# Where the moving operands of TensorE begin, modulo 128 bytes, in a two-layer fp32 block on one Trainium2 core

## The chip, the core and the metric

The kernel runs on one core of one Trainium2 chip (trn2). The metric is device microseconds of one execution: 2106.06 us is the median of three runs of the kernel before (2105.8 to 2108.58).

## The reference

Two layers on 256 tokens of width 2048, all in float32. Layer 0 is a convolution and pooling mixer and a swiglu, layer 1 a short-convolution mixer and a swiglu; an RMS norm ends it. Nearly all of the work is matrix products with weights that are each used once:

```python
def swiglu(h, w_gate, w_up, w_down):
    return (jax.nn.silu(h @ w_gate) * (h @ w_up)) @ w_down

    for i in range(DEPTH):
        ...
        if i % 2 == 0:
            h = h + conv_pool_mixer(h, ...)
        else:
            h = h + short_conv_mixer(h, ...)
        h = h + swiglu(rms_norm(h, ffn_norm[i]), w_gate[i], w_up[i], w_down[i])
    return rms_norm(h, final_norm)
```

The first mixer projects to 3072 features, runs a 31-tap causal convolution with a layer norm over 1024 of them and pooled averages over 1024, and projects back. The second projects to 6144 features, gates and convolves with 3 taps, and projects back. A swiglu has 5632 hidden features.

## The kernel before, in words

Activations lie with features on the partitions: a chunk is 128 features by 256 tokens, and the residual `h` has 16 chunks. The weights come as 128 x 128 blocks in the order of their use, from one array `in_wall`, in transfers of up to 16 blocks into the tiles `w`.

Every product is made in split precision. A weight piece of 8 blocks is rounded by ScalarE into `hi` (L114), and the rest, `w - hi`, goes into `lo` (L121, on VectorE, for part of the first mixer on GpSimd). `hi` and `lo` have 6 buffers each, and pieces are prepared 4 ahead of their use. An activation chunk is split alike by `split` (L193 to L200): it lies in 2 KB of a partition, 256 high values and then 256 low ones. For one weight block and one chunk, `product` issues in one of two forms:

- wide (all but the first mixer and the last chunk of the output): `hi` by all 512 columns of the chunk (L163), then `lo` by the 256 high ones (L164). This is called a pair here.
- narrow (the first mixer, and the last output chunk): `hi` by the 256 high values (L166), `hi` by the 256 low ones (L167), `lo` by the 256 high ones (L168). This is called a triple.

Each product loads its block of weights (512 bytes of each partition) into TensorE (PEld in the profile) and streams the chunk past it. Four tiles are streamed, the moving operands:

- `xs`, 16 chunks of normed input. It lives through the whole program and is written anew for each of the four stages that read it: the first mixer (M0; there it also takes the pooled branch's output, L200 from the pooling product), the first swiglu (F0), the second mixer (M1), the second swiglu (F1).
- `cat`, 8 chunks: in M0 first the pooled averages, later the layer-normed branch.
- `y`, 22 chunks: half of a swiglu's hidden features, filled and read twice in each swiglu.
- `z`, 16 chunks: the second mixer's gated values.

The stages follow each other: M0 (512 triples by `xs`, 144 by `cat`), F0 (`xs` 704 pairs, `y` 352, `xs` 704, `y` 352), M1 (`xs` 768, `z` 256), F1 (as F0, with the last 22 products of `y` as triples). In M0 the convolution's taps, the pooling and the layer norm run on VectorE, ScalarE and GpSimd beside the products, fed in by queues that count products. M0's last projection reads `cat` and waits for the layer norm; that norm's last steps stand in VectorE's order among the preparations of weights.

Tiles are placed by pools, one after the other in each partition: `h`, `xs`, then the four buffers of `w`, the six of `hi`, the six of `lo`, small ones, and last the tiles of the stage. So a tile that grows pushes those behind it.

Of the kernel before, what the change touches and what calls it, by code (L numbers as in the profile page):

```python
# [12 lines left out]
F32R = mybir.dt.float32r  # L13
# [4 lines left out]
P = 128  # L18
T = 256
D = 2048  # L20
NC = D // P
DC = 1024
NA = DC // P
FF = 5632
NF = FF // P
NH = NF // 2
# [46 lines left out]
WARM = 9  # L73

KEEP = 8

POOL_SPLIT = range(96, 24 * NC + 16 + 7 * NC + 8)

# [6 lines left out]
def block_kernel(ctx: ExitStack, tc: tile.TileContext, xT: bass.AP, xtok: bass.AP, vec: bass.AP, wall: bass.AP, out: bass.AP):  # L85
    nc = tc.nc
    const = ctx.enter_context(tc.tile_pool(name="const", bufs=1))
    act = ctx.enter_context(tc.tile_pool(name="act", bufs=1))
# [35 lines left out]
    def next_block():  # L124
        b, i = cursor
        at = UNIT_AT[PIECES[i][0]] + PIECES[i][1]
        if b == at + PIECES[i][2]:
            ready.pop(i)
            i, at = i + 1, b
        for j in range(i, i + LOOK + 1):  # L130
            prepare(j)
        if i + LOOK < len(PIECES):
            for u in range(PIECES[i + LOOK][0] + 1, PIECES[i + LOOK][0] + AHEAD + 1):
                fetch(u)
        cursor[:] = [b + 1, i]
        hi, lo = ready[i]
        o = (b - at) * P
        return hi[:, o : o + P], lo[:, o : o + P]
# [8 lines left out]
    def tick():  # L147
        for name, q in queues.items():
            credit[name] = credit[name] + 1.0 if q else 0.0
            while q and credit[name] >= PACE[q[0][0]]:  # L150
                cost, step = q.popleft()
                credit[name] -= PACE[cost]
                step()

    def drain():
        while any(queues.values()):
            for q in queues.values():
                if q:
                    q.popleft()[1]()

    def product(acc, hi, lo, x, first, last, wide):
        if wide:
            nc.tensor.matmul(acc, hi, x, start=first, stop=False, skip_group_check=True)  # L163
            nc.tensor.matmul(acc[:, T:], lo, x[:, :T], start=False, stop=last, skip_group_check=True)  # L164
        else:
            nc.tensor.matmul(acc[:, :T], hi, x[:, :T], start=first, stop=False)  # L166
            nc.tensor.matmul(acc[:, :T], hi, x[:, T:], start=False, stop=False)  # L167
            nc.tensor.matmul(acc[:, :T], lo, x[:, :T], start=False, stop=last)  # L168

    def matmul_chunks(xs, ks, n=1, wide=False, behind=None):  # L170


        accs = [ps.tile([P, 2 * T], F32, name="acc") for _ in range(n)]
        for i, k in enumerate(ks):
            first, last = i == 0, i == len(ks) - 1
            for acc in accs:
                hi, lo = next_block()
                product(acc, hi, lo, xs[:, k, :], first, last, wide)
                tick()
            if behind is not None:  # L180
                behind(k)
        return accs
# [10 lines left out]
    def split(dst, src, scale=None):  # L193

        if scale is None:
            nc.scalar.copy(dst[:, :T], src)
            nc.vector.tensor_tensor(out=dst[:, T:], in0=src, in1=dst[:, :T], op=ALU.subtract)
        else:
            nc.scalar.activation(dst[:, :T], src, AF.Copy, scale=scale)
            nc.vector.scalar_tensor_tensor(out=dst[:, T:], in0=src, scalar=scale, in1=dst[:, :T], op0=ALU.mult, op1=ALU.subtract)  # L200
# [4 lines left out]
    def col(name, i):  # L205
        return v[:, VECS[name] + i : VECS[name] + i + 1]

    identity = v[:, VECS["identity"] :]
    h = act.tile([P, NC, T], F32, name="h")
    xs = act.tile([P, NC, 2 * T], F32R, name="xs")  # L210
    ones = const.tile([P, P], F32, name="ones")
    nc.gpsimd.memset(ones, 1.0)

# [14 lines left out]
    def rsqrt_of(*totals, scale, halves=False, st=None):  # L228
# [9 lines left out]
        if halves:  # L238

            idle = ps.tile([P, P], F32, name="idle", tag="acc")  # L240
            with tc.issue_after(mm.ins):
                for _ in range(KEEP):
                    nc.tensor.matmul(idle, ones, ones, start=True, stop=True)  # L243
# [27 lines left out]
    class Norm:  # L271


        def __init__(self, gain, final=False):
            self.gain, self.final = gain, final
            self.sums = []

        def add(self, c):
# [6 lines left out]

        def scale(self, c):
            if not self.final:
                split(xs[:, c, :], h[:, c, :], col(self.gain, c))

        def square(self, c):  # L290
            if c == 0:
# [16 lines left out]
    def project(src, ks, norm=None, wide=False, narrow_end=False):  # L308

        for n in range(NC):  # L310
            if narrow_end and n == NC - 1:
                wide = False
            (acc,) = matmul_chunks(src, ks, wide=wide)
            if wide:
                t = phase[0].tile([P, T], F32, name="cross", bufs=3)
                nc.scalar.copy(t, acc[:, T:])
                nc.vector.tensor_tensor(out=h[:, n, :], in0=h[:, n, :], in1=t, op=ALU.add)
            nc.vector.tensor_tensor(out=h[:, n, :], in0=acc[:, :T], in1=h[:, n, :], op=ALU.add)  # L318
            if norm is not None:
                norm.add(n)  # L320

    def scaled(acc, r, name, wide=False):
        if not wide:
            s = (phase[0] if name == "pv" else tmp).tile([P, T], F32, name=name, bufs=2)
            nc.vector.tensor_tensor(out=s, in0=acc[:, :T], in1=r, op=ALU.mult)
            return s
        s = summed(acc, name)
        nc.vector.tensor_tensor(out=s, in0=s, in1=r, op=ALU.mult)
        return s


    norm = Norm("mix_norm_e")
    nc.sync.dma_start(v[:, :NC], vec[:, :NC])

    def load(at, n):
# [30 lines left out]
    every = range(NC)  # L366
    with tc.tile_pool(name="m0", bufs=1) as m0, tc.tile_pool(name="ps_side", bufs=2, space=PSUM) as ps_side:
# [1 line left out]
        a_in = m0.tile([P, NA, pad + T], F32, name="a_in")  # L369
        nc.gpsimd.memset(a_in[:, :, :pad], 0.0)  # L370
        conv = m0.tile([P, NA, T], F32, name="conv")
        cat = m0.tile([P, NA, 2 * T], F32R, name="cat")
        total = m0.tile([P, 2, T], F32, name="total")

        sides, prods, state = {}, {}, {}
# [156 lines left out]

        project(xs, POOL_CHUNKS)
        drain()
        norm = Norm("ffn_norm0")
        project(cat, range(NA), norm)

    def swiglu(norm, following):
        with tc.tile_pool(name="ffn", bufs=1) as fp:
            phase[0] = fp  # L540
            y = fp.tile([P, NH, 2 * T], F32R, name="y")
            r = None
            for half in range(2):
                for f in range(NH):
                    (acc_g,) = matmul_chunks(xs, every, wide=True)
                    (acc_u,) = matmul_chunks(xs, every, wide=True)
                    if r is None:
                        r = norm.rstd()
                    gate = scaled(acc_g, r, "gate", True)
                    up = scaled(acc_u, r, "val", True)  # L550
                    nc.scalar.activation(gate, gate, AF.Silu)
                    nc.vector.tensor_tensor(out=up, in0=up, in1=gate, op=ALU.mult)
                    split(y[:, f, :], up)
                project(y, range(NH), following if half else None, wide=True, narrow_end=half and following.final)
# [1 line left out]
    x0.close()  # L556


    after = Norm("mix_norm_o")
    swiglu(norm, after)  # L560


    norm = Norm("ffn_norm1")
    with tc.tile_pool(name="m1", bufs=1) as m1:
        phase[0] = m1
        z = m1.tile([P, NC, 2 * T], F32R, name="z")
        pad = SW - 1
        r = None
        for c in range(NC):
            (acc_c,) = matmul_chunks(xs, every, wide=True)  # L570
            (acc_v,) = matmul_chunks(xs, every, wide=True)
            if r is None:
                r = after.rstd()
            cg = scaled(acc_c, r, "gate", True)
            vv = scaled(acc_v, r, "val", True)
            cv = m1.tile([P, pad + T], F32, name="cv", bufs=2)
            nc.gpsimd.memset(cv[:, :pad], 0.0)
            nc.vector.tensor_tensor(out=cv[:, pad:], in0=cg, in1=vv, op=ALU.mult)
            wc = VECS["conv_w_o"] + c * SW
            co = m1.tile([P, T], F32, name="co", bufs=2)  # L580
            nc.vector.tensor_scalar(out=co, in0=cv[:, :T], scalar1=v[:, wc : wc + 1], scalar2=None, op0=ALU.mult)
            for k in range(1, SW):
                nc.vector.scalar_tensor_tensor(out=co, in0=cv[:, k : k + T], scalar=v[:, wc + k : wc + k + 1], in1=co, op0=ALU.mult, op1=ALU.add)
            (acc_b,) = matmul_chunks(xs, every, wide=True)
            bg = scaled(acc_b, r, "pv", True)
            nc.vector.tensor_tensor(out=bg, in0=bg, in1=co, op=ALU.mult)
            split(z[:, c, :], bg)
        project(z, every, norm, wide=True)


    last = Norm("final_norm", final=True)
    swiglu(norm, last)
    halves = rsqrt_of(*last.sums, scale=1.0 / D, halves=True)
    with tc.tile_pool(name="fin", bufs=1) as fin:

# [90 lines left out]
```

## Time and profile before

| | |
|---|---|
| median of three runs | 2106.06 us (2105.8 to 2108.58) |
| profiled execution | 2103.73 us, its span 2102.0 us |
| TensorE clock granted, mean | 0.997 of full |
| matmuls, weight loads | 12584 each |
| transfers | 395.53 MB, mean 188 GB/s |

The page gives busy time by engine, the chain of work that ended last, and groups of instructions by line and tile; times are microseconds unless marked ns. Matmuls are pipelined, and the duration of one reaches into the next. The view of one tile in a stretch gives for each line the count, the shortest, median and longest duration in ns, and the start of the first and of the last, in us from the span's start. The view of stretches gives for each engine the busy time and, in brackets, its instructions, then the clock, the share of the DMA engines and GB/s. The chain of waits gives start, duration and instruction.

### The profile page before, as it was taken

How to read it: one execution, taken by the hardware profiler on the slowest of the kernel's cores; microseconds unless marked ns; L12 is line 12 of the kernel's file. 1: busy time of each engine (PE TensorE's matmuls, PEld its weight loads, DVE VectorE, ACT ScalarE, POOL GpSimd, SP SyncE). 2: the span in 40 equal slices, each digit the busy share in tenths (PEclk: the TensorE clock that was granted, in tenths of full speed). 3: DMA queues.
4: the chain of work that ended last, by engine and by line, in shares of the span. 5: the costliest groups of instructions: out<-in, count | busy, mean ns of one | idle time of the engine just before them, and what ended most of it. 6: DMA issues, size and time to landing. Idle time of an engine off the chain costs nothing.

```text
span 2102.0 us, 31608 instructions
## 1 busy us (share of the span) xinstructions
PE 2079.1 (99%) x12584; PEld 1855.8 (88%) x12584; DVE 1383.4 (66%) x1979; ACT 1060.9 (50%) x1571; POOL 200.6 (10%) x180
## 2 busy tenths in 40 slices
PE   8999999999999999999999999999999999999998
PEld 8999988888888888888888888888888888888887
DVE  6888866666556666666777777666666556666654
ACT  7776654444444444454444445554444444444453
POOL 3985200000000000011000001100000000000011
PEclk9999999999999999999999999999999999999999
DMA  8554455555555555555555555555555555555551
GB/s 326 187 191 168 158 184 197 183 198 182 194 185 188 193 187 194 183 196 182 183 198 182 198 183 193 180 189 198 183 196 184 189 192 183 198 182 199 182 192 68
DMA packets 56884, 395.53 MB, mean 188 GB/s; under 512 B 6432, under 2 KB 7200, under 8 KB 9760
## 3 DMA queue, kind: packets, MB, share of 16 engines
q1 hardware_dynamic: 56736, 393.52, 52.4%
q8 instruction: 98, 1.61, 0.3%
q14 instruction: 50, 0.41, 0.1%
HBM read 391.39 MB, written 2.10 MB: 187 GB/s over the span
## 4 chain that ended last, share of the span: by engine, by line
PE 98%; DMA 1%; DVE 1%; ACT 0%; SPq 0%; issue 0%; DVEq 0%; ACTq 0%
PE acc L163 57%; PE acc L164 30%; PE acc L166 4%; PE acc L168 4%; PE acc L167 4%; DMA rows<-in_xtok 0%; DMA h<-in_xT 0%; DVE res L603 0%; ACT hi L114 0%; PE st L237 0%; PE st L268 0%; DVE lo L121 0%; SPq L104 0%; ACT conv L475 0%; PE idle L243 0%
## 5 line engine op out<-in xcount | busy, mean ns | idle before, releaser
L114 ACT CAST hi<-w 128x1024 fp32r<-128x1024 f32 (+1 forms) x740 | 776.1, 1050 | 975.3 <-PE acc L163 621.0
L121 DVE TENSOR_TENSOR lo<-w,hi 128x1024 fp32r<-128x1024 f32 (+1 forms) x691 | 845.2, 1224 | 639.5 <-ACT hi L114 635.3
L163 PE MATMUL acc<-xs,hi 128*128 128x512 f32 x3584 | 1243.3, 391 | 0.0
L164 PE MATMUL acc<-xs,lo 128*128 128x256 f32 x3584 | 1004.7, 280 | 0.0
L163 PEld LDWEIGHTS acc<-xs,hi 128*128 128x128 f32 x3584 | 670.4, 187 | 146.2
L164 PEld LDWEIGHTS acc<-xs,lo 128*128 128x128 f32 x3584 | 678.1, 189 | 0.1
L163 PE MATMUL acc<-y,hi 128*128 128x512 f32 x1386 | 485.2, 393 | 0.0
L164 PE MATMUL acc<-y,lo 128*128 128x256 f32 x1386 | 386.4, 279 | 0.0
L163 PEld LDWEIGHTS acc<-y,hi 128*128 128x128 f32 x1386 | 259.4, 187 | 61.7
L164 PEld LDWEIGHTS acc<-y,lo 128*128 128x128 f32 x1386 | 259.9, 187 | 0.4
L298 POOL TENSOR_TENSOR sumsq<-sumsq,sq 128x256 f32<-128x256 f32 x56 | 58.8, 1050 | 1599.1 <-ACT sq L296 1599.1
L166 PE MATMUL acc<-xs,hi 128*128 128x256 f32 x512 | 144.0, 284 | 5.2 <-ACT hi L114 4.2
L167 PE MATMUL acc<-xs,hi 128*128 128x256 f32 x512 | 143.6, 283 | 0.0
L168 PE MATMUL acc<-xs,lo 128*128 128x256 f32 x512 | 141.3, 284 | 0.1
L121 POOL TENSOR_TENSOR lo<-w,hi 128x1024 fp32r<-128x1024 f32 x49 | 118.7, 2441 | 43.1 <-PE acc L167 34.3
L166 PEld LDWEIGHTS acc<-xs,hi 128*128 128x128 f32 x512 | 98.1, 192 | 6.2 <-ACT hi L114 5.0
L167 PEld LDWEIGHTS acc<-xs,hi 128*128 128x128 f32 x512 | 98.2, 192 | 0.0
L168 PEld LDWEIGHTS acc<-xs,lo 128*128 128x128 f32 x512 | 96.5, 192 | 0.5 <-DVE lo L121 0.5
L163 PE MATMUL acc<-z,hi 128*128 128x512 f32 x256 | 89.6, 393 | 0.0
L188 ACT COPY cross<-acc 128x256 f32<-128x256 f32 x224 | 80.6, 360 | 0.0
L164 PE MATMUL acc<-z,lo 128*128 128x256 f32 x256 | 71.3, 279 | 0.0
L318 DVE TENSOR_TENSOR h<-acc,h 128x256 f32<-128x256 f32 x112 | 47.2, 423 | 18.9 <-PE acc L168 13.2
(134 smaller groups left out, 1198.6 us busy)
## 6 DMA issues: line engine op xcount, KB each, us to landing
w<-in_wall SPq DMA_DIRECT2D x365, 1024.0 KB, 4.8
w<-in_wall SPq DMA_DIRECT2D x7, 512.0 KB, 7.7
rows<-in_xtok SPq DMA_DIRECT2D x2, 1024.0 KB, 7.9
h<-in_xT SPq DMA_DIRECT2D x7, 256.0 KB, 7.3
out<-res SPq DMA_DIRECT2D x2, 512.0 KB, 2.8
out<-res SPq DMA_DIRECT2D x2, 384.0 KB, 2.8
v<-in_vec SPq DMA_DIRECT2D x1, 260.0 KB, 6.7
h<-in_xT SPq DMA_DIRECT2D x2, 128.0 KB, 2.3
```

Source lines behind the costliest of these rows:

```text
L114: nc.scalar.copy(hi[:, : n * P], w)
L121: engine.tensor_tensor(out=lo[:, : n * P], in0=w, in1=hi[:, : n * P], op=ALU.subtract)
L163: nc.tensor.matmul(acc, hi, x, start=first, stop=False, skip_group_check=True)
L164: nc.tensor.matmul(acc[:, T:], lo, x[:, :T], start=False, stop=last, skip_group_check=True)
L166: nc.tensor.matmul(acc[:, :T], hi, x[:, :T], start=first, stop=False)
L167: nc.tensor.matmul(acc[:, :T], hi, x[:, T:], start=False, stop=False)
L168: nc.tensor.matmul(acc[:, :T], lo, x[:, :T], start=False, stop=last)
L188: nc.scalar.copy(t, acc[:, T:])
L298: nc.gpsimd.tensor_tensor(out=self.sums[0], in0=self.sums[0], in1=sq, op=ALU.add)
L318: nc.vector.tensor_tensor(out=h[:, n, :], in0=acc[:, :T], in1=h[:, n, :], op=ALU.add)
```

## The change

Each of the four moving tiles gets 32 more elements (128 bytes) in each partition, and what the program reads and writes is a view in it that begins some bytes in: 0 or 32, one number for each tile and stage (`XS_M0` 32, `Y_F0`, `Y_F1` and `Z_M1` 32, all others 0). The views of `xs` for the stages lie in one tile, so M0's and F0's overlap shifted by 32 bytes.

```diff
+XS_M0 = 32
+XS_F0 = 0
+XS_M1 = 0
+XS_F1 = 0
+Y_F0 = 32
+Y_F1 = 32
+Z_M1 = 32
+CAT = 0
...
-    xs = act.tile([P, NC, 2 * T], F32R, name="xs")
+    xs_room = act.tile([P, NC * 2 * T + 32], F32R, name="xs")
+
+    def moving(room, at, n):
+
+        return room[:, at // 4 : at // 4 + n * 2 * T].rearrange("p (c t) -> p c t", c=n)
...
-        def __init__(self, gain, final=False):
+        def __init__(self, gain, at=0, final=False):
             self.gain, self.final = gain, final
+            self.xs = moving(xs_room, at, NC)
...
-                split(xs[:, c, :], h[:, c, :], col(self.gain, c))
+                split(self.xs[:, c, :], h[:, c, :], col(self.gain, c))
...
-    norm = Norm("mix_norm_e")
+    norm = Norm("mix_norm_e", XS_M0)
+    xs = norm.xs
...
-        cat = m0.tile([P, NA, 2 * T], F32R, name="cat")
+        cat = moving(m0.tile([P, NA * 2 * T + 32], F32R, name="cat"), CAT, NA)
...
-            y = fp.tile([P, NH, 2 * T], F32R, name="y")
+            y = moving(fp.tile([P, NH * 2 * T + 32], F32R, name="y"), at, NH)
...
-        z = m1.tile([P, NC, 2 * T], F32R, name="z")
+        z = moving(m1.tile([P, NC * 2 * T + 32], F32R, name="z"), Z_M1, NC)
```

The order of the instructions on each engine and the semaphores that they wait for are the same in both programs. What differs is the addresses. These are the bytes in each partition at which the tiles begin in the built programs; `hi`'s first buffer stands for all weights, since the buffers of `hi` and `lo` lie 4096 bytes apart. Distance is moving operand minus weights.

| operand | before | after | distance mod 128, before | after | distance mod 512, before | after |
|---|---|---|---|---|---|---|
| `hi` | 101696 | 101824 | | | | |
| `xs` in M0 | 36160 | 36192 | 0 | 32 | 0 | 416 |
| `xs` in F0, M1, F1 | 36160 | 36160 | 0 | 0 | 0 | 384 |
| `cat` | 184672 | 184800 | 32 | 32 | 32 | 32 |
| `y`, `z` | 159136 | 159296 | 96 | 0 | 96 | 128 |

More of the change, by code (lines that the diff above doesn't have):

```diff
@@ L534, in block_kernel, with swiglu @@
         drain()
-        norm = Norm("ffn_norm0")
+        norm = Norm("ffn_norm0", XS_F0)
         project(cat, range(NA), norm)
-    def swiglu(norm, following):
+    def swiglu(norm, following, at):
         with tc.tile_pool(name="ffn", bufs=1) as fp:
             phase[0] = fp
-            y = fp.tile([P, NH, 2 * T], F32R, name="y")
+            y = moving(fp.tile([P, NH * 2 * T + 32], F32R, name="y"), at, NH)
             r = None
@@ L544, in swiglu @@
                 for f in range(NH):
-                    (acc_g,) = matmul_chunks(xs, every, wide=True)
-                    (acc_u,) = matmul_chunks(xs, every, wide=True)
+                    (acc_g,) = matmul_chunks(norm.xs, every, wide=True)
+                    (acc_u,) = matmul_chunks(norm.xs, every, wide=True)
                     if r is None:
@@ L556, in block_kernel @@
     x0.close()
-    after = Norm("mix_norm_o")
-    swiglu(norm, after)
-    norm = Norm("ffn_norm1")
+    after = Norm("mix_norm_o", XS_M1)
+    swiglu(norm, after, Y_F0)
+    norm = Norm("ffn_norm1", XS_F1)
     with tc.tile_pool(name="m1", bufs=1) as m1:
         phase[0] = m1
-        z = m1.tile([P, NC, 2 * T], F32R, name="z")
+        z = moving(m1.tile([P, NC * 2 * T + 32], F32R, name="z"), Z_M1, NC)
         pad = SW - 1
@@ L569, in block_kernel @@
         for c in range(NC):
-            (acc_c,) = matmul_chunks(xs, every, wide=True)
-            (acc_v,) = matmul_chunks(xs, every, wide=True)
+            (acc_c,) = matmul_chunks(after.xs, every, wide=True)
+            (acc_v,) = matmul_chunks(after.xs, every, wide=True)
             if r is None:
@@ L583, in block_kernel @@
                 nc.vector.scalar_tensor_tensor(out=co, in0=cv[:, k : k + T], scalar=v[:, wc + k : wc + k + 1], in1=co, op0=ALU.mult, op1=ALU.add)
-            (acc_b,) = matmul_chunks(xs, every, wide=True)
+            (acc_b,) = matmul_chunks(after.xs, every, wide=True)
             bg = scaled(acc_b, r, "pv", True)
@@ L591, in block_kernel @@
     last = Norm("final_norm", final=True)
-    swiglu(norm, last)
+    swiglu(norm, last, Y_F1)
     halves = rsqrt_of(*last.sums, scale=1.0 / D, halves=True)
```

## The prediction

> **What bounds the kernel now.** I read the page first: the busy shares, the chain that ended last, and the costliest groups.
>
> ```profile
> span 2102.0 us, 31608 instructions
> PE 2079.1 (99%) x12584; PEld 1855.8 (88%) x12584; DVE 1383.4 (66%) x1979; ACT 1060.9 (50%) x1571; POOL 200.6 (10%) x180
> PE 98%; DMA 1%; DVE 1%; ACT 0%; SPq 0%; issue 0%; DVEq 0%; ACTq 0%
> L114 ACT CAST hi<-w 128x1024 fp32r<-128x1024 f32 (+1 forms) x740 | 776.1, 1050 | 975.3 <-PE acc L163 621.0
> L163 PE MATMUL acc<-xs,hi 128*128 128x512 f32 x3584 | 1243.3, 391 | 0.0
> L163 PE MATMUL acc<-y,hi 128*128 128x512 f32 x1386 | 485.2, 393 | 0.0
> L166 PE MATMUL acc<-xs,hi 128*128 128x256 f32 x512 | 144.0, 284 | 5.2 <-ACT hi L114 4.2
> L163 PE MATMUL acc<-z,hi 128*128 128x512 f32 x256 | 89.6, 393 | 0.0
> ```
>
> TensorE sets the end: 98% of the last chain is its own matmuls, the wide ones wait for nothing (idle 0.0), and ScalarE, which rounds the weights, spends 621 us waiting for matmuls to give buffers back. So the time moves only if a matmul's pace moves. The weight loads (PEld) fill 88% of the span: nearly always one reads weights while a matmul reads its moving operand. The change touches nothing but where these two reads lie against each other. The instructions of the two programs stand in the same order on every engine, with the same waits.
>
> The mean durations above (391, 393) overlap each other and are modelled, so I take paces from the view of one tile in one stage: its first and last start, and the count. In order: `xs` in the second half of the first swiglu, `y` behind its first half, `y` behind its second half, `z` in the second mixer, `xs` in the last half of the kernel.
>
> ```profile
> L163 PE MATMUL acc<-xs,hi x704: 390/391/396, 628.1 to 871.8; 128*128 128x512 f32 x176
> ...
> L163 PE MATMUL acc<-y,hi x352: 389/394/423, 504.9 to 627.8; 128*128 128x512 f32 x176
> ...
> L163 PE MATMUL acc<-y,hi x352: 389/394/422, 872.2 to 995.1; 128*128 128x512 f32 x176
> ...
> L163 PE MATMUL acc<-z,hi x256: 389/394/423, 1263.0 to 1352.3; 128*128 128x512 f32 x128
> ...
> L163 PE MATMUL acc<-xs,hi x704: 390/391/397, 1721.3 to 1965.0; 128*128 128x512 f32 x176
> ```
>
> Per wide pair (a 512-column product with hi, a 256-column product with lo): `xs` 243.7 us / 703 = 346.7 ns, twice; `y` 122.9 / 351 = 350.1 ns, twice; `z` 89.3 / 255 = 350.2 ns. Same instructions, same weight buffers, no waits. What differs is the tile: by the table of addresses above, `xs` begins at the weights' bytes modulo 128, `y` and `z` 96 bytes past them.
>
> The same view for the narrow triples (three products of 256 columns): `xs` in the first mixer, `cat` in its output projection, and the last 22 triples of `y`.
>
> ```profile
> L167 PE MATMUL acc<-xs,hi x303: 281/283/284, 41.1 to 149.8; 128*128 128x256 f32 x152
> ...
> L167 PE MATMUL acc<-cat,hi x96: 277/279/281, 225.9 to 259.2; 128*128 128x256 f32 x96
> ...
> L166 PE MATMUL acc<-y,hi x22: 279/282/285, 2080.9 to 2088.5; 128*128 128x256 f32 x22
> L167 PE MATMUL acc<-y,hi x22: 279/282/286, 2081.1 to 2088.6; 128*128 128x256 f32 x22
> ```
>
> `xs`, at distance 0: 108.7 / 302 = 359.9 ns a triple. `cat`, at distance 32: 33.3 / 95 = 350.5 ns. `y`, at 96: between 7.5 / 21 = 357 and 7.6 / 21 = 362 ns. So the best place depends on the form: distance 0 beats 96 for pairs, 32 beats 0 and 96 for triples. That `y` narrow, in a stage with GpSimd at rest, is no faster than `xs` speaks against the load of the other engines as the cause of `cat`'s pace. This trace therefore holds every combination of form and distance that the change makes, and each edit can be priced from a row.
>
> **The change, part by part.** *y to distance 0.* 1386 pairs go from 350.1 to 346.7: 1386 x 3.5 ns (122.9/351 - 243.7/703) = 4.8 us. The 22 narrow triples go from 357 to 362 to 359.9 ns: under 0.1 us either way, nothing.
>
> *z to distance 0.* 256 x 3.5 ns = 0.9 us. Both lie wholly on TensorE's path, and all 1642 pairs count: 5.7 us.
>
> *xs of the first mixer to distance 32.* There are 512 such triples, at 359.9 - 350.5 = 9.4 ns each. Not all count. These rows count the later ones, and the chain of waits shows what came before:
>
> ```profile
> L168 PE MATMUL acc<-xs,lo x32: 283/283/284, 27.8 to 38.9; 128*128 128x256 f32 x32
> ...
> L168 PE MATMUL acc<-xs,lo x128: 279/283/365, 158.4 to 205.9; 128*128 128x256 f32 x128
> ```
>
> ```profile
> 12.48 9.11 DMA rows<-in_xtok
> 21.61 1.32 ACT rows L349
> ...
> 25.86 0.75 PE acc L168 x4
> ```
>
> 303 + 128 + 32 = 463 triples run after the input has landed; the first 49 stand in the stretch where the chain is a transfer (9.11 us) and what follows it, so their saving, 49 x 9.4 = 0.5 us, is swallowed. 463 x 9.4 = 4.4 us. The distance of 32 has no row with `xs` itself; I take `cat`'s 350.5 because form, distance and weight buffers are the same. The bounds are that pace and, for a loss, the slowest pace of a triple in these rows, 362: 463 x 2.1 ns = 1.0 us the other way.
>
> Will the rest of the first mixer follow? It is the one place where other engines are nearly full:
>
> ```profile
> 41.00:150.00 109.00, 109.00 (x909) 109.00 (x910) 96.64 (x181) 86.57 (x154) 101.01 (x56) 1.00 0.53 186
> ```
>
> TensorE would pass this stretch in 109.0 - 303 x 9.4 ns = 106.2 us. VectorE needs 96.6 and GpSimd 101.0 of them (columns after the two of TensorE), so both still fit, and weights are prepared four pieces ahead. Then come two stalls of TensorE, at 150 to 157 and, longer, here:
>
> ```profile
> 205.93 0.13 PE acc L167
> 206.14 1.05 ACT hi L114
> 207.22 1.23 DVE lo L121
> 208.44 0.41 DVE diag L260 x2
> ...
> 212.70 0.52 ACT cat L477
> 213.26 1.44 PE acc L166 x5
> ```
>
> The chain into `cat` starts at a matmul: ScalarE's rounding waits for that matmul's weight buffer, VectorE's `lo` for the rounding, and the layer norm's steps stand behind `lo` in VectorE's order. If the matmuls end earlier, the stall begins and ends earlier, at its old length of 7 us. So I let the 4.4 us through.
>
> *xs of the three later stages* (offset 0) stays at distance 0: 3584 pairs at 346.7, no change. `cat` (offset 0) stays at 32. ScalarE and VectorE write `xs`, `y`, `z` at other bytes; should that cost them something, they have 975 us (the idle time before ScalarE's rounding) to hide it in.
>
> Sum: 5.7 + 4.4 = 10.1 us. The profiled execution took 2103.7 us (2102.0 of span), 2.3 below the median of the three timed runs, 2106.06, and would take 2093.6. Taken off the median: 2096.0.
>
> **The rivals.** *The distance counts modulo 256 or 512 (slower).* The rows can't tell 128 from these: the weight blocks lie 512 bytes apart, the chunks of a moving tile 2048 apart, and the pace is the same for all of them, so the period divides 512, no more. And `xs`'s spare bytes push all weight buffers 128 bytes up: modulo 256 and 512 the pairs of `xs`, 3584 of 5226, would no longer stand at distance 0, nor would `y` and `z` arrive there. If these 3584 pairs took the pace of `y`, and `y` and `z` kept it, the loss is 3584 x 3.5 = 12.5 us and the gain of 5.7 is gone; with the first mixer unchanged that gives 2118.6. It decides from 10.1 / 3584, some 2.8 ns a pair. For it: nothing excludes it. Against it: the two steps seen (0 and 96, 0 and 32) come from distances under 128, and 1% of pace turns on 32 bytes. Chance 0.11.
>
> *The first mixer gives nothing.* VectorE or GpSimd, at 89% and 93% in 41 to 150, fall behind, or `cat`'s pace belongs to its stage and not to its 32 bytes. Then 5.7 us are left: 2100.4. Against it stand the narrow `y` row and the sum of the stretch above. Chance 0.12.
>
> *No change at all.* The paces belong to the stages and not to the bytes (in `y`'s stages the residual is updated beside the matmuls, in `xs`'s not): 2106.1. Against it: `z` and `y` agree to 0.1 ns in stages of 16 and 22 chunks, while the `xs` stages, whose other work is that of swiglu or of the mixer, agree as well. Beside this stands a rule of the Trainium skill: SBUF — State Buffer, Who interferes with whom, gives TensorE two independent read ports, one for the moving operand and one for the weights, and says that it never waits on anyone; TensorE: Matmul & The Clock Gate, Back-to-back issue gap, gives N/2.4 + 2.5 ns for a warm matmul, which makes an estimate of 325 ns for a pair. By that rule no placement could matter and the time would stay 2106.1; the trace disagrees with it, since the pairs take 346.7 and 350.1 ns without a wait. Chance 0.06.
>
> **How the numbers follow.** The forecast has 0.71: 2096.0. A measurement of this kernel can tell about 0.2%, 4 us, from no change; the forecast (-10.1) and the second rival (-5.7) are both beyond that, so faster has 0.71 + 0.12 = 0.83, same 0.06, slower 0.11. The range holds the first two cases: below, all 512 triples count (0.5 us more) and the run falls 2.3 us under the median as the profiled one did, 2096.0 - 2.8 = 2093.2; above, the second rival with the first mixer's 1.0 us of loss, 2101.4.
>
> **What would show it.** In the profile after, `y` and `z` should run at 346.7 ns a pair, 243.7 us for 703 pairs of `xs` should stand as before, and the first mixer's triples should fall from 359.9 to 350.5. The stage of `y` from 504.9 should take 1.2 us less. If `xs`'s wide pairs move at all, the period isn't 128 and the forecast is wrong. If the triples quicken but the stall ahead of `cat` grows by as much, the second rival is right.

## The result, and the profile after

The changed kernel takes 2121.06 us (median of four runs, 2119.15 to 2122.9) against 2106.59 for the kernel before: 1.0070 of it, with an interval of 1.0057 to 1.0084. The forecast was 2096.0, faster; it is slower by 14.5 us, outside the range. The rival that ends on the other side had given 2118.6 and a chance of 0.11.

The page of the profile after: span, engines, the chain by engine, and the two largest groups of 512-column matmuls (lines are 10 further down than before: L173 and L174 are the wide pair, L176 to L178 the narrow triple).

```profile
span 2121.1 us, 31608 instructions
PE 2098.9 (99%) x12584; PEld 1869.4 (88%) x12584; DVE 1383.8 (65%) x1979; ACT 1061.3 (50%) x1571; POOL 200.4 (9%) x180
PE 98%; DVE 1%; DMA 0%; ACT 0%; SPq 0%; issue 0%; DVEq 0%; ACTq 0%
...
L173 PE MATMUL acc<-xs,hi 128*128 128x512 f32 x3584 | 1259.1, 394 | 0.0
...
L173 PE MATMUL acc<-y,hi 128*128 128x512 f32 x1386 | 486.5, 393 | 0.0
```

Still TensorE, 98% of the chain, the wide matmuls without a wait. The other engines have the work and the busy times of before. So again only the pace can have moved. The view of one tile in one stage, after, in the order: `xs` in the second half of the first swiglu, `y` behind its first half, `z`, and the triples of `xs` in the first mixer.

```profile
L173 PE MATMUL acc<-xs,hi x703: 387/396/398, 633.5 to 879.9; 128*128 128x512 f32 x176
...
L173 PE MATMUL acc<-y,hi x351: 387/396/400, 509.9 to 632.7; 128*128 128x512 f32 x176
...
L173 PE MATMUL acc<-z,hi x256: 387/396/398, 1275.2 to 1364.7; 128*128 128x512 f32 x128
...
L177 PE MATMUL acc<-xs,hi x303: 282/283/283, 42.2 to 151.0; 128*128 128x256 f32 x152
```

`xs`: 246.4 / 702 = 351.0 ns a pair, where it was 346.7. `y`: 122.8 / 350 = 350.9, and `z`: 89.5 / 255 = 351.0, where they were 350.1 and 350.2. (Taken from the starts to the nanosecond, without interrupted pairs, all ten stages of pairs run at 351.1.) The triples: 108.8 / 302 = 360.3 ns, where they were 359.9; the hoped-for 350.5 is not there. (The 128 triples of `xs` that follow from 159.5 us run at 356, without interrupted ones, where they were 359.9: 0.5 us in all.)

So where did the time go? 3584 pairs of `xs` x 4.4 ns = 15.8 us, 1642 pairs of `y` and `z` x 1.0 = 1.6 us, and the first pair of all starts at 261.4 us instead of 259.5, 1.9 us: 19.3 us by these terms, against 19.1 between the two spans (2121.1 - 2102.0). The 1.9 us need no cause in the change: w_shift256 below, whose triples of `xs` run at 360.0 as before and whose time is that of before, starts its first pair at 262.3. This profiled execution is the longest of its four, so the medians differ by less. The largest term is the tile whose own bytes the change left where they were: what moved were the weights, 128 bytes up, behind `xs`'s spare bytes.

### The profile page after: what moved, and what is told of

Same layout as the page of the kernel before. It is cut to its first block, busy times and chain, and to the rows that moved or that the text cites. A ratio compares the mean times of both kernels' runs of the same rounds, so it can differ in the third digit from the quotient of the medians.

```text
span 2121.1 us, 31608 instructions
## 1 busy us (share of the span) xinstructions
PE 2098.9 (99%) x12584; PEld 1869.4 (88%) x12584; DVE 1383.8 (65%) x1979; ACT 1061.3 (50%) x1571; POOL 200.4 (9%) x180
## 4 chain that ended last, share of the span: by engine, by line
PE 98%; DVE 1%; DMA 0%; ACT 0%; SPq 0%; issue 0%; DVEq 0%; ACTq 0%
PE acc L173 57%; PE acc L174 30%; PE acc L176 4%; PE acc L177 4%; PE acc L178 4%; DMA w<-in_wall 0%; DVE res L620 0%; ACT hi L124 0%; PE st L252 0%; PE st L283 0%; ACT conv L492 0%; PE idle L258 0%; DVE conv L447 0%; SPq L114 0%; SPq L353 0%
## 5 line engine op out<-in xcount | busy, mean ns | idle before, releaser
L173 PE MATMUL acc<-xs,hi 128*128 128x512 f32 x3584 | 1259.1, 394 | 0.0
L174 PE MATMUL acc<-xs,lo 128*128 128x256 f32 x3584 | 1014.3, 283 | 0.0
L173 PEld LDWEIGHTS acc<-xs,hi 128*128 128x128 f32 x3584 | 673.2, 188 | 155.3
L174 PEld LDWEIGHTS acc<-xs,lo 128*128 128x128 f32 x3584 | 673.8, 188 | 0.1
L173 PE MATMUL acc<-y,hi 128*128 128x512 f32 x1386 | 486.5, 393 | 0.0
L174 PE MATMUL acc<-y,lo 128*128 128x256 f32 x1386 | 391.3, 283 | 0.0
L173 PEld LDWEIGHTS acc<-y,hi 128*128 128x128 f32 x1386 | 260.1, 188 | 59.8
L174 PEld LDWEIGHTS acc<-y,lo 128*128 128x128 f32 x1386 | 260.6, 188 | 0.4
L176 PE MATMUL acc<-xs,hi 128*128 128x256 f32 x512 | 145.0, 286 | 4.6 <-ACT hi L124 3.6
L178 PE MATMUL acc<-xs,lo 128*128 128x256 f32 x512 | 141.5, 285 | 0.0
L176 PEld LDWEIGHTS acc<-xs,hi 128*128 128x128 f32 x512 | 98.7, 193 | 5.5 <-ACT hi L124 4.2
L178 PEld LDWEIGHTS acc<-xs,lo 128*128 128x128 f32 x512 | 96.7, 193 | 0.0
L173 PE MATMUL acc<-z,hi 128*128 128x512 f32 x256 | 89.9, 394 | 0.0
L174 PE MATMUL acc<-z,lo 128*128 128x256 f32 x256 | 72.2, 283 | 0.0
```

## The experiments

Theory A at first: the distance from the weights to the moving operand counts, with a period longer than 128 bytes. Against it B, the weights' own start modulo 256, and C, something else in the views. After the first four runs A became H: the distance modulo 256 sets which rhythms of matmul and weight load can hold, and the rhythm in which a stage is entered picks among them. Against it P: the operands' own start modulo 256. All kernels but one have TensorE's instructions in the order of the kernel before. (Where an unused tile is added, GpSimd clears it once.)

**w_shift**: the shift of the weights alone, in the kernel before.

```diff
     xs = act.tile([P, NC, 2 * T], F32R, name="xs")
+    gap = act.tile([P, 32], F32, name="gap")
+    nc.gpsimd.memset(gap, 0.0)
```

> The kernel before with an unused tile of 128 bytes between xs and the weights: weights and everything behind them move up by 128 bytes, no moving operand is a view. Theory A, the distance from weights to moving operand counts, with a period longer than 128 bytes: the pairs of xs (now at distance 384 modulo 512) go from 346.7 to 351.1 ns as in the changed kernel, y and z keep distance 96 and 350.1 ns; 3584 x 4.4 ns = 15.8 us, total near 2122. Theory B, the weights' own start modulo 256 counts: y and z go to 351 as well, total near 2124. Theory C, the distance counts modulo 128 and the loss came from the views or the 32 bytes: nothing changes, 2106.6.

It took 2119.69 us, 1.0064 of before (1.0049 to 1.0079): nearly all of the loss, with no view in it. `xs` in the second half of the first swiglu and `y` ahead of it:

```profile
L163 PE MATMUL acc<-xs,hi x703: 387/396/400, 631.3 to 877.8; 128*128 128x512 f32 x176
...
L163 PE MATMUL acc<-y,hi x352: 392/394/396, 508.1 to 631.0; 128*128 128x512 f32 x176
```

`xs` 246.5 / 702 = 351.1, `y` 122.9 / 351 = 350.1, its pace of before, though the weights it meets moved as far. That excludes C, since nothing here is a view, and B with it: the same weights are slower only for the operand that did not move along.

**xs_late**: the changed kernel with the late views of `xs` moved up after the weights.

```diff
-XS_F0 = 0
-XS_M1 = 0
-XS_F1 = 0
+XS_F0 = 128
+XS_M1 = 128
+XS_F1 = 128
```

> The changed kernel with XS_F0, XS_M1 and XS_F1 128 instead of 0: the pairs of xs are back at distance 0 modulo 512, weights, y, z and the first mixer stay where the change put them. Theory A: the pairs of xs run at 346.7 ns again, 3584 x 4.4 = 15.8 us less than the changed kernel, total near 2105.3. Theory B: they stay at 351 ns, total near 2121. Theory C: no change, 2121.

It took 2128.16 us, 1.0101 of before (1.0084 to 1.0118). No theory had that: at distance 0 `xs` ran slower than at 384.

```profile
L173 PE MATMUL acc<-xs,hi x703: 395/398/403, 632.8 to 880.8; 128*128 128x512 f32 x176
```

248.0 / 702 = 353.3 ns a pair. Distance alone doesn't set the pace, and A in its simple form falls.

**map1** and **map2**: each stage its own distance.

```diff
-XS_M0 = 32
+XS_M0 = 64
 XS_F0 = 0
-XS_M1 = 0
-XS_F1 = 0
-Y_F0 = 32
+XS_M1 = 32
+XS_F1 = 64
+Y_F0 = 0
 Y_F1 = 32
-Z_M1 = 32
-CAT = 0
+Z_M1 = 64
+CAT = 128
...
-    xs_room = act.tile([P, NC * 2 * T + 32], F32R, name="xs")
+    xs_room = act.tile([P, NC * 2 * T + 128], F32R, name="xs")
```

(The other tiles get 128 elements too; map2 is the same with other numbers.)

> All four moving tiles get 512 spare bytes, and each stage its own distance (moving operand minus weights, modulo 512): pairs at 0 (xs F0), 32 (xs M1), 64 (xs F1), 96 (y F0), 128 (y F1), 160 (z); triples at 64 (xs in the first mixer) and 160 (cat). Theory A: 0 gives 346.7, 96 gives 350.1 and 128 gives 351.1 ns a pair whichever tile stands there; 32, 64 and 160 are not known. Theory B: all pairs alike, near 347 to 350, since the weights' start modulo 512 is that of the kernel before.

> As the first map with other distances: pairs at 192 (xs F0), 224 (xs M1), 256 (xs F1), 288 (y F0), 320 (y F1), 352 (z); triples at 128 (xs in the first mixer) and 224 (cat). Theory A with a period of 256: 256 gives 346.7 like 0, 352 gives 350.1 like 96, 288 and 320 give what the first map shows at 32 and 64. Theory A with a period of 512: these differ. Theory B: all pairs alike.

They took 2112.27 and 2119.72 us in one run each. `y` in the last swiglu of map1, at 128:

```profile
L173 PE MATMUL acc<-y,hi x352: 387/396/400, 1601.4 to 1724.6; 128*128 128x512 f32 x176
```

123.2 / 351 = 351.0 (351.1 from the starts to the nanosecond, without interrupted pairs): 128 gave what 384 had given. 96 and 352 gave 350.0 in all stages, 32 and 288 gave 346.7: the period is 256 as far as it shows. 351.1 at 128 stands on weights that begin at 64 modulo 256 here and at 192 in the changed kernel and w_shift, so there the weights' own start makes no difference. But 256 itself gave two paces in one kernel, in the two halves of the last swiglu, at the same bytes:

```profile
L173 PE MATMUL acc<-xs,hi x644: 391/391/391, 1384.9 to 1607.8; 128*128 128x512 f32 x161
...
L173 PE MATMUL acc<-xs,hi x694: 395/398/403, 1734.9 to 1979.8; 128*128 128x512 f32 x174
```

222.9 / 643 = 346.7 in the first half, 244.9 / 693 = 353.4 in the second. The same instructions with the same operands: what differs is what ran before. The second half follows `y` at distance 320, the first half `z` at 352 and a break (below). This is what made theory H.

**w_shift256**: as w_shift, with `gap` 64 elements wide (256 bytes).

> As w_shift with an unused tile of 256 bytes instead of 128: xs at distance 256, y and z at 96, the first mixer's xs at 256. With a period of 256 bytes: everything as before, pairs of xs at 346.7 ns, total 2106.6. With a period of 512: the pairs of xs at another pace, most likely 353.3 as in one stage of the second map, total near 2130.

It took 2106.4 us, 1.0003 of before (0.9994 to 1.0012). `xs` in the second half of the first swiglu:

```profile
L163 PE MATMUL acc<-xs,hi x704: 390/391/397, 631.2 to 874.9; 128*128 128x512 f32 x176
```

243.7 / 703 = 346.7. A shift of 256 costs nothing where one of 128 cost 13 us: the period is 256 bytes, not 128 and not 512.

**all_shift**: the gap of 128 bytes ahead of `xs`, so that every distance stays.

```diff
+    gap = act.tile([P, 32], F32, name="gap")
+    nc.gpsimd.memset(gap, 0.0)
     xs = act.tile([P, NC, 2 * T], F32R, name="xs")
```

> The kernel before with an unused tile of 128 bytes ahead of xs: xs, weights, y, z and cat all move up by 128 bytes, and every distance stays what it was before. Theory H, the distance modulo 256 sets which rhythms of matmul and weight load can hold, and the rhythm in which a stage is entered picks among them: nothing changes, pairs of xs 346.7 ns, y and z 350.1, total 2106.6. Theory P, the operands' own start modulo 256 counts: xs at 192 as in xs_late gives 353.1 ns, 3584 x 6.4 = 23 us more, total near 2130.

It took 2118.01 us, 1.0057 of before (1.0041 to 1.0073): between the theories. The second half of the first swiglu kept its pace; the second mixer's `xs` lost it, but not at once:

```profile
L163 PE MATMUL acc<-xs,hi x704: 390/391/397, 632.5 to 876.3; 128*128 128x512 f32 x176
...
L163 PE MATMUL acc<-xs,hi x714: 387/398/403, 1019.9 to 1271.8; 128*128 128x512 f32 x179
```

243.8 / 703 = 346.8 in the former, 251.9 / 713 = 353.3 in the latter. The timeline of TensorE in the second mixer shows the point at which it turns:

```profile
1013.93 0.39 PE L163 MATMUL acc<-xs,hi 128*128 128x512 f32 x1
...
1018.43 0.40 PE L163 MATMUL acc<-xs,hi 128*128 128x512 f32 x1
...
1018.78 0.40 PE L163 MATMUL acc<-xs,hi 128*128 128x512 f32 x1
1019.01 0.60 PE L270 MATMUL st<-diag,ones 128*128 128x256 f32 x2
1019.26 0.47 PE L164 MATMUL acc<-xs,lo 128*128 128x256 f32 x1
...
1020.26 0.40 PE L163 MATMUL acc<-xs,hi 128*128 128x512 f32 x1
...
1023.79 0.40 PE L163 MATMUL acc<-xs,hi 128*128 128x512 f32 x1
```

From 1013.93 to 1018.43 there are 13 pairs, 4.50 / 13 = 346 ns each; from 1020.26 to 1023.79 there are 10, 353 each. Between stands the spreading of the token scale (L270 here), a float32 product that falls in the middle of a pair. To the nanosecond the gaps between pairs alternate 350 and 343 ns ahead of it, and from 1020.26 on they repeat 350, 361 and 349: this is what is called a rhythm here. The slow one holds for the some 700 pairs that are left of the stage. In the three stages of `xs` with such a break the pairs after it run at 353.3, in the two without it at 346.7.

**no_break**: all_shift without that break in the last two of the three. In the second mixer and the second swiglu the kernel leaves out the whole token scale and takes that of the first swiglu. So eight small float32 products are gone too, which add up the scale's squares and which stand 8 us ahead of the spreading.

```diff
                     if r is None:
-                        r = norm.rstd()
+                        r = first_r[0] if first_r else norm.rstd()
+                        first_r[:] = [r]
...
             if r is None:
-                r = after.rstd()
+                r = first_r[0]
```

> all_shift, but the second mixer and the second swiglu take the first swiglu's token scale instead of computing their own (their scale is left out, so their values differ): the small float32 products that interrupt the pairs of xs 32 pairs into a stage, some 2 us with their wait, are gone there. Theory H with a break as what moved the rhythm: the pairs of xs in the second mixer and in the first half of the second swiglu enter from z or y at distance 96 in the fast rhythm and keep it, 346.7 instead of 352.9 ns; 1472 x 6.2 ns = 9.1 us, and some 3 us for the breaks: 2118.0 - 12 = 2106. The first half of the first swiglu keeps its break and its 352.9. Theory P: only the breaks' 3 us go, 2115.

It took 2106.88 us, 1.0006 of before (0.9997 to 1.0015), against H's 2106 and P's 2115. The same part of the second mixer:

```profile
L163 PE MATMUL acc<-xs,hi x734: 390/391/392, 1011.7 to 1265.8; 128*128 128x512 f32 x184
```

254.1 / 733 = 346.7 at the same bytes as in all_shift. The first swiglu's first half, which kept its break, stayed at 353.3. That leaving out the token scale's products keeps the fast pace is shown. The timeline above points at the spreading, since the pace was still 346 ns behind the eight products; they changed the gaps, from 347 throughout to 350 and 343 in turn, and whether the spreading alone would turn the rhythm was not tried. What decides to which it turns is not shown either: after the spreading at distance 0 all seven stages with weights that begin at 192 modulo 256 (xs_late, all_shift, and the one break left in no_break) ran on at 353.3, and ten of eleven with weights at 64 (before, w_shift256, the maps, as_meant) at 346.7. So P's variable, the operands' own start, may have a part in it; this is a count over kernels that differ in more than that, and no test.

**as_meant** and **all32**: the change as the prediction priced it, and one distance for all. Both give each moving tile 128 spare elements and set the offsets so that the distances modulo 512 are, for as_meant, 0 for `xs`, `y` and `z` and 32 for the first mixer's `xs` and `cat`, and for all32, 32 throughout. The numbers of all32 (as_meant has 0 for the late `xs` and 416 for `y` and `z`):

```diff
-XS_F0 = 0
-XS_M1 = 0
-XS_F1 = 0
-Y_F0 = 32
-Y_F1 = 32
-Z_M1 = 32
+XS_F0 = 32
+XS_M1 = 32
+XS_F1 = 32
+Y_F0 = 448
+Y_F1 = 448
+Z_M1 = 448
```

> What the prediction took the change to do, made real modulo 512: xs of the later stages, y and z at distance 0, the first mixer's xs and cat at 32 (512 spare bytes in each moving tile). The prediction's prices: pairs of y and z 346.7 ns instead of 350.1 (5.7 us), triples 350 instead of 359.9 (4.4 us), total 2096. Theory H: distance 0 can hold 346.7 or 353.3, and no stage of pairs changes the distance, so all 5226 pairs run in whichever rhythm the first stages leave: 2096, or 2096 + 5226 x 6.6 ns = 2130, or a mixture.

> All moving operands at distance 32 modulo 512, first mixer included (512 spare bytes in each). In the two maps 32, 160 and 288 ran at 346.7 to 346.8 ns a pair in every stage, whatever came before. Theory H: all 5226 pairs at 346.7, triples at 350 as cat: 1642 x 3.4 + 463 x 9.4 ns = 10 us below before, total 2096.7. If 32 too has a slow rhythm, some stages stand at 350 or more and the total lies above 2100.

as_meant took 2104.0 us, 0.9996 of before (0.9983 to 1.0008), so no difference that shows. A mixture is what came, in the one execution that was profiled: it is seen in `y` behind the two halves of the first swiglu. The first mixer's triples ran as priced:

```profile
L173 PE MATMUL acc<-y,hi x352: 391/392/397, 501.0 to 622.7; 128*128 128x512 f32 x176
...
L173 PE MATMUL acc<-y,hi x350: 392/398/403, 867.8 to 991.0; 128*128 128x512 f32 x175
...
L177 PE MATMUL acc<-xs,hi x300: 277/280/282, 41.0 to 145.7; 128*128 128x256 f32 x150
```

121.7 / 351 = 346.7 in the first, 123.2 / 349 = 353.0 in the second; the triples 104.7 / 299 = 350.2 ns. The second `y` entered at 346.7 and turned some 25 pairs later, with no float32 product near:

```profile
875.08 0.40 PE L173 MATMUL acc<-y,hi 128*128 128x512 f32 x1
875.32 0.28 PE L174 MATMUL acc<-y,lo 128*128 128x256 f32 x1
875.43 0.39 PE L173 MATMUL acc<-y,hi 128*128 128x512 f32 x1
875.66 0.27 PE L174 MATMUL acc<-y,lo 128*128 128x256 f32 x1
875.78 0.62 PE L173 MATMUL acc<-y,hi 128*128 128x512 f32 x2
876.24 0.40 PE L174 MATMUL acc<-y,lo 128*128 128x256 f32 x2
876.47 0.40 PE L173 MATMUL acc<-y,hi 128*128 128x512 f32 x1
```

From there on:

```profile
L173 PE MATMUL acc<-y,hi x324: 395/398/403, 876.8 to 991.0; 128*128 128x512 f32 x162
```

114.2 / 323 = 353.6, and 353.3 from the starts to the nanosecond. At 875.78 two pairs stand interleaved, `hi`, `hi`, `lo`, `lo`. Every kernel here has this place once in each of the five stages of `y` and `z`. At distance 0, in as_meant, it turned the pace in three of the five: twice from 346.7 to 353.3 and once, at 1606.6, from 353.3 to 346.7. At 64 and at 80 it changed the pace in one stage each, at 32, 96, 128 and 160 in none. So another step out of the order of pairs can turn a stage too, and not the spreading alone.

all32 took 2096.07 us, 0.9949 of before (0.993 to 0.9969). Its pairs run at 346.7 in all ten stages, but the triples, at the same bytes and distances as in as_meant, take 108.0 / 300 = 360.0 ns:

```profile
L173 PE MATMUL acc<-y,hi x352: 390/390/398, 505.0 to 626.7; 128*128 128x512 f32 x176
...
L176 PE MATMUL acc<-xs,hi x301: 283/283/283, 40.9 to 148.9; 128*128 128x256 f32 x151
```

So the triples at 32 have more than one rhythm as well, and the trace of before had shown one of them for `cat`.

**all32_m64**: all32 with the first mixer's `xs` at 64.

```diff
-XS_M0 = 32
+XS_M0 = 64
```

> all32 with the first mixer's xs at distance 64 instead of 32. There all32 ran at 360 ns a triple for most of the stage although as_meant ran at 350 with the same addresses; the first map ran at 353.3 at 64. If 64 holds 353.3: 330 triples x 6.6 ns = 2.2 us less than all32, 2094; pairs stay at 346.7. If 64 also has a rhythm of 360: 2096.

It took 2093.84 us, 0.9943 of before (0.993 to 0.9957), the fastest version tried: pairs at 346.7 in all stages, and triples of `xs` at 106.7 / 302 = 353.3:

```profile
L177 PE MATMUL acc<-xs,hi x303: 278/279/282, 41.1 to 147.8; 128*128 128x256 f32 x152
```

**fine**: a third map between the steps of 32; the edit is that of map1 with other numbers.

> A third map, between the steps of 32 (modulo 256): pairs at 16 (xs F0), 48 (xs M1), 144 (xs F1), 176 (y F0), 80 (y F1), 8 (z); triples at 16 (xs in the first mixer) and 48 (cat). Paces seen so far are 346.7, 349, 350.0, 351.1 and 353.3 ns a pair; theory H expects these steps again and not values in between, with 16 and 8 near those of 0 and 32. A pace under 346.7 would be a better place than any so far.

2104.53 us in one run. 16 and 144 gave 346.7, 80 and 176 gave 350.0, 48 gave 351.1, and 8 gave 353.3: again those steps and nothing in between or below, but not in the order of the distances, since 8 lies between 16 and 0, where 346.7 was seen.

## Why the prediction was wrong, step by step

*What bounds the kernel* held: TensorE's own pace, 98% of the chain in both profiles, and no wait where none was.

*"stays at distance 0: 3584 pairs at 346.7, no change"*, said of `xs` in the three later stages, is the step that failed, and with it the sign. It stood on distances modulo 128. w_shift and w_shift256 show the period to be 256: 128 bytes cost 13 us, 256 nothing. Modulo 256 the change sent 3584 pairs from 0 to 128, 351.1 ns, 15.8 us.

*"y to distance 0"* and *"z to distance 0"*, 5.7 us: they never arrived there. By the same period they came to 128, and lost 1.0 ns a pair instead of gaining 3.5. Where they did stand at a place with 346.7, in all32, the price was right.

*"xs of the first mixer to distance 32"*, 4.4 us: it came to 160 modulo 256 and ran at 360, the last 128 triples at 356. The price was right where it did come to 32 and fell into the rhythm of `cat`: in as_meant the first pair starts at 255.4 us, and in the four traces with triples at 360 and distances of before (before, w_shift256, all_shift, no_break) at 259.5 to 262.3. That at least 4.1 us arrive of the 4.4 also bears out the step on VectorE, GpSimd and the two stalls, which let the saving through.

*"This trace therefore holds every combination of form and distance that the change makes, and each edit can be priced from a row"* failed twice: by the period, and because a row shows one rhythm out of several. Even the change as meant gave 2104.0, not 2096.0.

*The first rival* was right in its mechanism: 2118.6 against 2121.06. That its price came so close is in part luck, since it had borrowed 350.1 from `y` for a place that no row showed, and the pairs ran at 351.1. Its chance was set too low. The argument against it, that steps under 128 bytes make a difference, says that the period is above 32 and nothing on whether it ends at 128, and "nothing excludes it" was the stronger half. The table of the front had the distances modulo 512 beside those modulo 128, and every place in use changed in it but `cat`.

*The rule of the Trainium skill*: SBUF — State Buffer, Who interferes with whom, gives TensorE independent read ports for the moving operand and for the weights, and says that it never waits on anyone. TensorE: Matmul & The Clock Gate, Back-to-back issue gap, gives N/2.4 + 2.5 ns, by its words for an isolated matmul, which makes an estimate of 325 ns for the pair. That placement makes no difference, as the prediction drew from this, is not borne out here: with the same instructions and no idle time before them the pair took 346.7 to 353.3 ns, by the place of its two operands and what ran before.

## What to carry to other kernels

Where an effect depends on an address, work out what every operand's distance becomes modulo more than the period that is assumed, the unmoved ones too: padding one tile moves all tiles behind it. A pace that the trace shows for one place is the pace of one rhythm; before pricing other stages by it, look whether all stages at that place share it, and whether something interrupts them. A place whose pace is the same in every stage and after every break (32 for pairs here) is worth more than a place that is as fast in some.

## What the runs showed of the hardware that was not expected

- Back-to-back pairs of matmul and weight load settle into rhythms that hold for hundreds of pairs. Their means are few: 346.7, 350.0, 351.1 and 353.3 ns for 768 columns in two products (349 in a single stage).
- Which of them can hold depends on the distance from weights to moving operand modulo 256 bytes. For pairs: 346.7 at 16, 32, 144 and 160; 350.0 at 80, 96 and 176 (at 80 after a start at 353 in one stage); 351.1 at 48 and 128; 353.3 at 8, 192 and 224; two paces each at 0 (346.7 and 353.3) and at 64 (353.3 in three stages and the start of a fourth, 349 in the rest of that one). Several of these stand on one kernel.
- At distance 0 a stage turned from 346.7 to 353.3, for the rest of its 250 us, where a short float32 product stood between two pairs, and in as_meant where only two pairs were interleaved. Entered from `y` or `z` at 96 without the float32 products, it stayed at 346.7 each time. What selects the rhythm was not settled. `diag` moved with the weights and `ones` did not, which was not tried apart; the turns in as_meant's `y` need neither of them.
